# Weight sums of the query, key and gate products made beside the products, in three token blocks in place of two

## The chip, the cores and the metric

The kernel runs on one core of a Trainium2 chip. The metric is the time of one execution on the device in microseconds (us); lower is better. The engines of the core are TensorE (PE in the profile, with its weight loads as PEld), VectorE (DVE), ScalarE (ACT), GpSimd (POOL) and SyncE (SP), whose queue issues all the DMAs here.

## The reference

One inference step of two layers over 2048 prompt tokens and 64 sample tokens (8 requests of 8 tokens). The change lies in layer 1, the retention layer:

```python
p = _rmsnorm(x, norm_w) @ w_in                       # (L,1024) @ (1024,6144)
q, k, v, gate = jnp.split(p, [1024, 2048, 4096], axis=-1)
q = _rotary(q.reshape(B, L, 4, 256), pos0)
k = _rotary(k.reshape(B, L, 4, 256), pos0) * 256 ** -0.5
v = v.reshape(B, L, 4, 512)
o, S = _retention_chunked(q, k, v, S0)               # per head: S = s_dec*S + k^T v, o = q S + (q k^T * D) v
o = _rmsnorm(o, onorm_w) * jax.nn.silu(gate.reshape(B, L, 4, 512))
y = x + o.reshape(B, L, 2048) @ w_out                # then a final rmsnorm
```

Layer 0 (gated delta rule) runs before it and is not touched.

## The kernel before

Layer 1 takes the prompt in four blocks of 512 tokens (n = 0 to 3), and in each block the four heads (h = 0 to 3) one after the other; block 0 carries the 64 sample tokens along. I call the work of one block and head a stage, (n,h). A stage has, in program order: the gate, query and key products, the rotation of query and key, the value product, the output product of the stage before (`flush_B`, `outproj_B`), and then a task `ret_prompt` is added to a planner `pipe`. `pipe.pump()`, called between products, lets such tasks emit their next instructions; so the chain of head h (four chunks of 128 tokens, `kT`, `ap`, `o`, `p` on PE, with the state `Sr` between chunks) runs among the products of the next stage. In block 0 a second task `ret_sample` follows each `ret_prompt`: it fans out the sample values `vraw` by eight DMAs, makes a key tile `K3`, and works through 16 states that are loaded, updated (`ps` on PE, then DVE) and stored. The tile framework sets each engine's final order at build time; an engine then takes its instructions strictly in that order.

Every matrix product is made of three passes of rounded numbers: a weight is split into a high part (a copy on ACT, `L210`) and a low part (a subtraction on DVE, `L211`).

Blocks 0 and 1 make plain products: eight weight loads of 512 KB for gate, query and key, four for the values. Blocks 2 and 3 (`n >= FIRST7`) make each 2x2 block product from seven products of quarters (`quad`, `vquad`, `seven`) in place of eight. For that the tokens' side needs sums of quarters (`build_halves`, DVE and ACT) and the weights' side four sums for each of six weight pairs and head. `prep` makes these sums during blocks 0 and 1: 2 x 24 units, each with a load (`Rw`), four sums on POOL (`Sm`), a split on ACT and DVE, and two stores into the DRAM buffer `wh_d`. `wstream` then delivers the seven weight quarters of a product in the order of its job numbers x: 0, 1, 3 are plain quarters (loaded into `wraw` and split), 4 to 7 are the sums (loaded from `wh_d` straight into a weight tile). A weight tile holds two quarters and there are three of them, so the weights run at most six products ahead. At the end of block 1 the program waits in the planner for the rest of `prep` (`pipe.wait(*ptask)`) and then builds the halves of block 2.

Tiles with one tag share buffers in program order: the later one waits until the last reader of the earlier one is done. `p0`, `p1`, `p2` are such tags. In block 0 `p2` holds `vraw` and then `K3`; from block 1 on `p0` to `p2` serve as extra buffers for `xr`, the residual of the output product. `wraw` has two buffers.

Of the kernel before, what the change touches and what calls it, by code (L numbers as in the profile page):

```python
# [10 lines left out]
F32 = mybir.dt.float32  # L11
F32R = mybir.dt.float32r
AF = mybir.ActivationFunctionType
ALU = mybir.AluOpType
# [5 lines left out]
BH = 4  # L20
# [61 lines left out]
class _Layer:  # L82
    pb = None
# [8 lines left out]
def tile_hybrid(ctx: ExitStack, tc: tile.TileContext, a: dict, S: int):  # L92
    nc = tc.nc
    V, ACT, PL = nc.vector, nc.scalar, nc.gpsimd
# [47 lines left out]
    x1_d = dr.tile([D, S + NS], F32, name="x1_d")  # L142
    x2_d = dr.tile([D, S + NS], F32, name="x2_d")
    sr_d = dr.tile([BH, 128, 1024], F32, name="sr_d")
    wh_d = [dr.tile([24, 128, 1024], F32, name=f"wh_d{h}") for h in range(BH)]

    def const(name, shape, src, pool=cst):
        t = pool.tile(list(shape), F32, name=name)
# [26 lines left out]

    def xst(name, wide=True):
        if not wide and xn_[1] == 6:
            k = xn_[2] % 6
            xn_[2] += 1
            if k >= 3:  # L180
                return B.pb.tile([128, TB], F32, tag=f"p{k - 3}", name=name)
        else:
            k = xn_[0] % min(xn_[1], 3 if B.pb else 4)
            xn_[0] += 1
        return (pa if k == 3 else sb).tile([128, XC], F32, tag=f"xst{k}", name=name)
# [829 lines left out]
    def quarters(src, vkind):  # L1015

        if vkind:
            q = [[v3(src[j], 512)[:, :, 256 * i : 256 * i + 256] for i in range(2)] for j in range(2)]
            return q[0][0], q[1][0], q[0][1], q[1][1]
        return [src[j][:, 512 * i : 512 * i + 512] for j in range(2) for i in range(2)]  # L1020
# [16 lines left out]
    def prep(u):  # L1037

        pb = B.pb
        tag = ("ta", "tb")[u]  # L1040
        for h, t in ((h, t) for h in range(BH) for t in range(6)):
            src, vkind = quads(h)[t]
            R = pb.tile([128, 4, 256], F32R, tag=tag, bufs=2, name="Rw")
            Sm = pb.tile([128, 4, 256], F32, tag=tag, bufs=2, name="Sm")
            A11, A12, A21, A22 = (R[:, i, :].bitcast(F32) for i in range(4))
            for x, y in zip((A11, A12, A21, A22), halves_of(src, vkind, u)):
                nc.sync.dma_start(x, y)
            yield 10.0
            PL.tensor_tensor(Sm[:, 0], A21, A22, op=ALU.add)
            PL.tensor_tensor(Sm[:, 1], Sm[:, 0], A11, op=ALU.subtract)  # L1050
            PL.tensor_tensor(Sm[:, 2], A11, A21, op=ALU.subtract)  # L1051
            PL.tensor_tensor(Sm[:, 3], A12, Sm[:, 1], op=ALU.subtract)
            yield 10.0
            with behind():
                ACT.copy(R, Sm)
                V.tensor_tensor(Sm.bitcast(F32R), Sm, R.bitcast(F32), op=ALU.subtract)
            yield 8.0
            out = wh_d[h][4 * t : 4 * t + 4].rearrange("x p (l v c) -> p x l v c", l=2, v=2)[:, :, :, u, :]
            nc.sync.dma_start(out[:, :, 0], R.bitcast(F32))
            nc.sync.dma_start(out[:, :, 1], Sm)  # L1060
            yield 8.0

    def wstream(h):

        q = quads(h)
        jobs = []
        for ts in ([0], [1], [2], [3], [4, 5]):
            for x in (0, 4, 5, 1, 6, 7, 3):
                jobs += [(t, x) for t in ts]
        for i in range(0, len(jobs), 2):  # L1070
            w, raw = wtile(), None
            for j, (t, x) in enumerate(jobs[i : i + 2]):
                o = w[:, j, :]
                src, vkind = q[t]
                if x < 4:
                    if raw is None:
                        raw = sb.tile([128, 1024], F32, tag="wraw", bufs=2, name="wraw")
                    d = raw[:, 512 * j : 512 * j + 512]
                    nc.sync.dma_start(v3(d, 256) if vkind else d, quarters(src, vkind)[x])
                    split(o[:, :512], o[:, 512:], d)  # L1080
                else:
                    nc.sync.dma_start(o.bitcast(F32), wh_d[h][4 * t + x - 4])
            for j in range(2):
                yield v3(w[:, j, :], 512)

# [38 lines left out]
    def seven(product, c):  # L1124

        add = lambda e, out, x, y: e.tensor_tensor(out, x, y, op=ALU.add)  # L1126
        ACT.copy(c[0][0], product("b11"))
        ACT.copy(c[1][1], product("t1"))
        add(V, c[0][1], product("t2"), c[0][0])
        add(V, c[0][0], product("b21"), c[0][0])  # L1130
        add(V, c[1][0], product("t3"), c[0][1])
        add(PL, c[0][1], c[0][1], c[1][1])
        add(PL, c[1][1], c[1][0], c[1][1])
        add(V, c[0][1], product("b22"), c[0][1])
        add(V, c[1][0], product("n4"), c[1][0])
# [47 lines left out]
    def ret_prompt(n, h, QR, KR, Vt, GT, OG, S_):  # L1183
        pb = B.pb
        gC = float(gam[h] ** 128)
        rmask = pb.tile([128, 128], F32, tag="rmk", bufs=2, name="rmk")
        nc.sync.dma_start(rmask, a["rmask"][:, h, :])
        for c in range(4):
            tk = slice(c * 128, (c + 1) * 128)
# [56 lines left out]
    def ret_sample(h, QRs, KRs, vraw, GTs, OG):  # L1246
# [52 lines left out]
        for half in range(2):  # L1299
# [31 lines left out]
            on = ret_on(o, h, 2)  # L1331

            def fin(oT, half=half):
                og = pb.tile([128, 4, 32], F32, tag="ogs", name="ogs")
                V.tensor_tensor(og.rearrange("p d (g t) -> p d g t", t=8),
                                oT.rearrange("p d (g s) -> p d g s", s=32)[:, :, :, 0:8],
                                GTs[:, :, 32 * half : 32 * half + 32].rearrange("p d (g t) -> p d g t", t=8),
# [231 lines left out]


PIN = False
FIRST7 = 2
LAT_E = 4.0
LAT_SUB = 51.0
LAT_K = 5.5
# [123 lines left out]
```

## Time and profile before

| | us |
|---|---|
| median of 3 runs | 3385.2 (3381.08 to 3391.85) |
| the profiled execution, its own time | 3395.24 |
| its span from the first to the last instruction | 3393.5 |
| layer 1 stages from (0,3)'s output product to the end | 1951.2 to 3393.5 |

The span is 1.7 us shorter than the execution's own time. Times of the trace are counted from the start of the span. A stage is bounded below by where the output product in it ends on PE, since PE is the engine that is nearly always busy.

### The profile page before, as it was taken

What the parts mean: (1) busy time and instruction counts of PE and PEld (TensorE: products, weight loads), DVE (VectorE), ACT (ScalarE), POOL (GpSimd) and SP (SyncE); (2) the same over time, 40 slices, a digit from 0 to 9 for tenths busy, and PEclk for the clock granted to TensorE, in tenths of its full rate; (3) what the DMA queues carried; (4) which work ended last, traced back from release to release, by engine and by line L of the source; (5) the groups of instructions that cost most, each with busy time, mean ns of one, the idle gap of its engine ahead of it and who ended that gap; (6) DMA issues with size and microseconds to landing.
All of it is one profiled execution on the core that took longest, in us unless ns stands there. A gap on an engine that the chain in (4) does not pass through costs nothing.

```text
span 3393.5 us, 57080 instructions
## 1 busy us (share of the span) xinstructions
PE 3216.8 (95%) x20572; PEld 2769.3 (82%) x20572; DVE 2357.0 (69%) x5218; ACT 1563.8 (46%) x3527; POOL 493.7 (15%) x770
## 2 busy tenths in 40 slices
PE   7999999999999999999999999999969999999997
PEld 6999887778788788788878778688759899889896
DVE  6876878687868868666475766666667567775666
ACT  7655564465435546335243443344344344443443
POOL 1221010001010000011113121222211111011110
PEclk9999999999999999999999999999979999999999
DMA  4333544335443333446767768766678867688665
GB/s 134 94 98 90 175 139 140 125 97 164 128 133 111 95 117 97 139 131 214 246 212 232 238 217 273 244 208 204 199 247 276 273 226 251 228 269 277 222 238 173
DMA packets 408650, 625.60 MB, mean 184 GB/s; under 512 B 119840, under 2 KB 237360, under 8 KB 408368
## 3 DMA queue, kind: packets, MB, share of 16 engines
q1 hardware_dynamic: 408368, 621.96, 57.3%
q8 instruction: 162, 2.65, 0.3%
q14 instruction: 120, 0.98, 0.1%
HBM read 473.04 MB, written 146.68 MB: 183 GB/s over the span
## 4 chain that ended last, share of the span: by engine, by line
PE 66%; DVE 10%; DMA 10%; ACT 6%; issue 4%; POOL 3%; SPq 1%; DVEq 0%; POOLq 0%; ACTq 0%
PE pp L101 37%; PE sq L101 5%; PE pv L101 5%; PE o L101 4%; PE p L101 4%; PE sv L101 3%; PE kyd L101 2%; DMA w<-wh_d 1%; DMA wraw<-in_w_qkg 1%; PE oT L110 1%; DMA x_d<-xr 1%; DVE w L197 1%; DMA wraw<-in_w_v 1%; POOL so L587 1%; DMA out_ret_s<-st 1%
## 5 line engine op out<-in xcount | busy, mean ns | idle before, releaser
L101 PE MATMUL pp<-xn,w 128*128 128x288 f32 (+1 forms) x6224 | 1285.6, 354 | 12.6 <-ACT xn L210 4.7
L101 PEld LDWEIGHTS pp<-xn,w 128*128 128x128 f32 x6224 | 993.4, 189 | 156.2 <-issue 19.3
L101 PE MATMUL pp<-OG,w 128*128 128x512 f32 (+1 forms) x2880 | 589.8, 363 | 35.4 <-DVE xr L1359 28.0
L101 PEld LDWEIGHTS pp<-OG,w 128*128 128x128 f32 x2880 | 487.9, 192 | 119.6 <-DVE xr L1359 28.0
L196 ACT CAST w<-wraw 128x1024 fp32r<-128x1024 f32 x320 | 336.6, 1052 | 383.6 <-PE pp L101 201.5
L197 DVE TENSOR_TENSOR w<-wraw,w 128x1024 fp32r<-128x1024 f32 x320 | 403.0, 1260 | 149.9 <-ACT w L196 141.0
L101 PE MATMUL sq<-xn,w 128*128 128x256 f32 x1536 | 206.2, 284 | 5.8 <-DVE GT L1126 3.3
L101 PEld LDWEIGHTS sq<-xn,w 128*128 128x128 f32 x1536 | 191.4, 188 | 10.4 <-issue 3.8
L101 PE MATMUL pv<-w,xn 128*128 128x512 f32 x768 | 188.5, 398 | 1.9 <-ACT w L196 1.7
L1359 DVE TENSOR_TENSOR xr<-xr,pp 128x512 f32<-128x512 f32 (+1 forms) x160 | 92.4, 592 | 133.6 <-PE pp L101 114.2
L101 PEld LDWEIGHTS pv<-w,xn 128*128 128x128 f32 x768 | 144.2, 189 | 39.5 <-ACT w L196 1.9
L743 DVE SCALAR_TENSOR_TENSOR acc<-pp,cw,acc 128x511 f32<-128x511 f32 (+2 forms) x216 | 160.3, 742 | 20.8 <-ACT acc L740 20.4
L210 ACT CAST w<-wraw 128x512 fp32r<-128x512 f32 x144 | 86.1, 623 | 151.7 <-PE pp L101 50.2
L211 DVE TENSOR_TENSOR w<-wraw,w 128x512 fp32r<-128x512 f32 x144 | 96.9, 688 | 46.7 <-ACT w L210 46.6
L101 PE MATMUL o<-Sc,Qc 128*128 128x512 f32 x360 | 103.1, 411 | 9.0 <-DVE Sc L211 4.7
L1051 POOL TENSOR_TENSOR Sm<-Rw 128x256 f32<-128x256 f32 x48 | 44.0, 917 | 463.9 <-DMA Rw<-in_w_qkg 302.4
L488 DVE TENSOR_TENSOR VP<-VP,tm 128x66 f32<-128x66 f32 (+26 forms) x510 | 106.6, 209 | 4.4
L486 DVE TENSOR_TENSOR tm<-LP,VP 128x66 f32<-128x66 f32 (+26 forms) x510 | 104.6, 205 | 6.1 <-DMA LP<-sl 2.1
L101 PE MATMUL p<-Vh,Kt 128*128 128x512 f32 x384 | 106.7, 409 | 0.7 <-ACT Vh L210 0.7
L1171 POOL TENSOR_TENSOR so<-oss,rsc 128x1 f32<-128x1 f32 x72 | 19.7, 274 | 562.0 <-ACT on L1169 562.0
L110 PE MATMUL oT<-ident,on 128*128 128x128 f32 x432 | 74.7, 280 | 26.8 <-DVE on L588 11.8
L210 ACT CAST OG<-og 128x256 fp32r<-128x256 f32 x192 | 71.7, 405 | 58.8 <-DVE og L643 27.6
(434 smaller groups left out, 5440.5 us busy)
## 6 DMA issues: line engine op xcount, KB each, us to landing
w<-wh_d SPq DMA_DIRECT2D x192, 512.0 KB, 5.6
wraw<-in_w_in_a SPq DMA_DIRECT2D x128, 512.0 KB, 3.5
x_d<-xr SPq DMA_DIRECT2D x160, 256.0 KB, 3.2
wraw<-in_w_qkg SPq DMA_DIRECT2D x64, 512.0 KB, 4.4
xr<-x_d SPq DMA_DIRECT2D x128, 256.0 KB, 4.4
wraw<-in_w_out_b SPq DMA_DIRECT2D x64, 512.0 KB, 4.1
wh_d<-Rw SPq DMA_DIRECT2D x48, 512.0 KB, 3.2
wh_d<-Sm SPq DMA_DIRECT2D x48, 512.0 KB, 3.5
```

The lines of the kernel that those rows point to most:

```text
L101: ins = nc.tensor.matmul(out, lhsT, rhs, start=start, stop=stop)
L110: ins = nc.tensor.transpose(out, x, ident[:p, :p])
L196: ACT.copy(w[:, 0, :], raw)
L197: V.tensor_tensor(w[:, 1, :], raw, w[:, 0, :].bitcast(F32), op=ALU.subtract)
L210: ACT.copy(hi, x)
L211: V.tensor_tensor(lo, x, hi.bitcast(F32), op=ALU.subtract)
L486: V.tensor_tensor(tv, LP[:, m, m + 1 : m + 1 + n].unsqueeze(2).to_broadcast([128, n, ncol]), VP[:, m, 0:ncol].unsqueeze(1).to_broadcast([1 ...
L488: V.tensor_tensor(VP[:, m + 1 : m + 1 + n, 0:ncol], VP[:, m + 1 : m + 1 + n, 0:ncol], tv, op=ALU.subtract)
L587: PL.tensor_tensor(so, so, mhalf[:, :2], op=ALU.pow)
L743: V.scalar_tensor_tensor(acc[:, sh:], ap[:, : TB - sh], cw[:, ct, j : j + 1], acc[:, sh:], op0=ALU.mult, op1=ALU.add)
L1051: PL.tensor_tensor(Sm[:, 2], A11, A21, op=ALU.subtract)
L1359: V.tensor_tensor(xs[:, s:e], xs[:, s:e], p[:, : e - s], op=ALU.add)
```

## The change

Three things happen. `FIRST7` goes from 2 to 1, so block 1 makes seven products as well. `prep` is cut to the two value pairs (t = 4, 5), 2 x 8 units. And the sums for gate, query and key are no longer stored: `wstream` loads a weight pair into the two `wraw` buffers, makes the sums on POOL into two tiles `P` (tags `p2` and `raws`) and in place in `wraw`, and splits all seven quarters on ACT and DVE, for every head of every block anew. In the order of the seven products the two that use plain weight quarters (x = 0 and 1) now come first, and `seven` adds in another order. Three buffers are given up (the second of `rmk`, the one of `ogs`, and `p2` as a buffer for `xr`).

```diff
-    wh_d = [dr.tile([24, 128, 1024], F32, name=f"wh_d{h}") for h in range(BH)]
+    wh_d = [dr.tile([8, 128, 1024], F32, name=f"wh_d{h}") for h in range(BH)]
...
-            k = xn_[2] % 6
+            k = xn_[2] % 5
...
-        for h, t in ((h, t) for h in range(BH) for t in range(6)):
+        for h, t in ((h, t) for h in range(BH) for t in (4, 5)):
...
-            for x in (0, 4, 5, 1, 6, 7, 3):
+            for x in (0, 1, 4, 5, 6, 7, 3):
                 jobs += [(t, x) for t in ts]
+        live = {}
+
+        def ready(t):
+
+            r = [sb.tile([128, 1024], F32, tag="wraw", bufs=2, name="wraw") for _ in range(2)]
+            for x, y in zip(r, q[t][0]):
+                nc.sync.dma_start(x, y)
+            P = [B.pb.tile([128, 512], F32, tag=x, name="P") for x in ("p2", "raws")]
+            A11, A12, A21, A22 = quarters(r, False)
+            PL.tensor_tensor(P[0], A21, A22, op=ALU.add)
+            PL.tensor_tensor(P[1], P[0], A11, op=ALU.subtract)
+            PL.tensor_tensor(A21, A11, A21, op=ALU.subtract)
+            live[t] = {0: A11, 4: P[0], 5: P[1], 1: A12, 6: A21, 7: P[0], 3: A22}
+
+        ready(0)
...
-                if x < 4:
+                if not vkind:
+                    split(o[:, :512], o[:, 512:], live[t][x])
+                    if x == 4:
+                        PL.tensor_tensor(live[t][7], live[t][1], live[t][5], op=ALU.subtract)
+                    if x == 3 and t < 3:
+                        ready(t + 1)
+                elif x < 4:
...
-        ACT.copy(c[0][0], product("b11"))
+        ACT.copy(c[1][0], product("b11"))
+        add(V, c[0][0], product("b21"), c[1][0])
         ACT.copy(c[1][1], product("t1"))
-        add(V, c[0][1], product("t2"), c[0][0])
-        add(V, c[0][0], product("b21"), c[0][0])
+        add(V, c[0][1], product("t2"), c[1][0])
...
-        rmask = pb.tile([128, 128], F32, tag="rmk", bufs=2, name="rmk")
+        rmask = pb.tile([128, 128], F32, tag="rmk", bufs=1, name="rmk")
...
-                og = pb.tile([128, 4, 32], F32, tag="ogs", name="ogs")
+                og = pb.tile([128, 4, 32], F32, tag="A", name="ogs")
...
-FIRST7 = 2
+FIRST7 = 1
```

How the order on the engines moves is seen at three places. The first is PE early in stage (1,0), where `ret_prompt` of (0,3) runs. Before, its chunks (`kT`, `ap`, `o`, `p`) stand between plain products (`pp`):

```order
L101 MATMUL pp_21846<-xn_21511,w 128x512 x3
L101 MATMUL pp_21847<-xn_21511,w 128x512 x3
L101 MATMUL o<-Vh,Ah 128x512 x3
L101 MATMUL p<-Vh,Kt 128x512 x6
L110 MATMUL kT<-ident,KR 128x128 x2
L101 MATMUL ap<-QR,KR 128x128 x2
L101 MATMUL pp_21846<-xn_21511,w 128x512 x3
L101 MATMUL pp_21847<-xn_21511,w 128x512 x3
```

In the changed kernel, at the same place, PE has the first two quarter products (`sq`, 24 matmuls, weights x = 0 and 1), and then the chunks:

```order
L101 MATMUL sq<-xn_21431,w 128x256 x6
L101 MATMUL sq<-xn_21432,w 128x256 x6
L101 MATMUL o<-Vh,Ah 128x512 x2
L101 MATMUL p<-Vh,Kt 128x512 x4
L101 MATMUL ap<-QR,KR 128x128 x2
L110 MATMUL oT<-ident,on 128x128 x3
L101 MATMUL o<-Sc,Qc 128x512
L110 MATMUL oT<-ident,on 128x128
L101 MATMUL o<-Sc,Qc 128x512 x5
L101 MATMUL o<-Vh,Ah 128x512 x3
L101 MATMUL p<-Vh,Kt 128x512 x6
L110 MATMUL kT<-ident,KR 128x128 x2
```

The plain products between the chunks are gone, and so it goes on for 31 rows, of which the last two are the first `os` of `ret_sample`: the third quarter product, whose weight x = 4 is a POOL sum, stands behind all four chunks.

The second place is POOL at the same time. In the changed kernel it has the `so` steps of the chunks of (0,3) (two rows each), the last two of which are shown, and behind them the sums for the first weight pair and the next (`P` and `wraw`):

```order
L1192 TENSOR_TENSOR so<-oss,rsc 128x1
L1193 TENSOR_TENSOR so<-so,mhalf 128x1
L1079 TENSOR_TENSOR P<-wraw 128x512
L1080 TENSOR_TENSOR P<-P,wraw 128x512
L1081 TENSOR_TENSOR wraw<-wraw 128x512
L1093 TENSOR_TENSOR P<-wraw,P 128x512
```

Before, the sums of `prep` (`Sm`) stand there, and no product of block 1 reads them:

```order
L1052 TENSOR_TENSOR Sm<-Rw,Sm 128x256
L1172 TENSOR_TENSOR so<-so,mhalf 128x1
L1171 TENSOR_TENSOR so<-oss,rsc 128x1
L1172 TENSOR_TENSOR so<-so,mhalf 128x1
L1171 TENSOR_TENSOR so<-oss,rsc 128x1
L1172 TENSOR_TENSOR so<-so,mhalf 128x1
L1051 TENSOR_TENSOR Sm<-Rw 128x256
```

So the first sum that block 1 needs has moved behind the last `so` of the chain of (0,3).

The third place is PE later in (1,0), where `ret_sample` of (0,3) updates its states (`os`, `ps`). In the changed kernel the fourth weight pair begins there:

```order
L101 MATMUL sq<-xn_21432,w 128x256 x5
L101 MATMUL os<-st,QRs 32x512 x4
L101 MATMUL sq<-xn_21432,w 128x256
L101 MATMUL ps<-V_22320,Kts 128x512 x2
L110 MATMUL oT<-ident,on 128x128 x4
L101 MATMUL ps<-V_22320,Kts 128x512 x2
L101 MATMUL os<-st,QRs 32x512 x4
L101 MATMUL ps<-V_22320,Kts 128x512 x4
L101 MATMUL sq<-xn_21429,w 128x256 x2
L101 MATMUL sq<-ta,w 128x256 x2
```

Before, the same instructions stand singly among plain products:

```order
L101 MATMUL ps<-V_22213,Kts 128x512
L101 MATMUL pp<-xn_21498,w 128x512
L101 MATMUL ps<-V_22213,Kts 128x512
L101 MATMUL pp<-xn_21498,w 128x512 x3
L101 MATMUL ps<-V_22213,Kts 128x512
L101 MATMUL pp<-xn_21498,w 128x512 x2
L101 MATMUL pp<-xn_21511,w 128x512
L101 MATMUL os<-st,QRs 32x512 x3
```

What moved: the third product of the fourth pair (`sq<-xn_21429` with a summed weight) now stands behind 15 of the 16 state updates, of which the last eight have no products between them.

## Rows read from the trace of the kernel before

**Rows 1.** The page: busy time, share of the span, instructions, by engine.

```profile
PE 3216.8 (95%) x20572; PEld 2769.3 (82%) x20572; DVE 2357.0 (69%) x5218; ACT 1563.8 (46%) x3527; POOL 493.7 (15%) x770
```

**Rows 2.** Windows, (1,0) to (3,0): us; busy PE, PEld, DVE, ACT, POOL; clock; DMA; GB/s.

```profile
1951.20:2111.30 160.10, 153.81 (x852) 126.93 (x851) 100.66 (x161) 66.27 (x121) 26.41 (x36) 1.00 0.75 245
2111.30:2233.70 122.40, 114.11 (x487) 89.58 (x486) 72.47 (x106) 44.89 (x74) 30.47 (x38) 0.96 0.73 236
2233.70:2341.60 107.90, 107.90 (x486) 87.30 (x485) 66.74 (x93) 43.97 (x73) 23.85 (x30) 1.00 0.65 212
2341.60:2506.70 165.10, 131.85 (x566) 103.75 (x565) 112.60 (x179) 71.28 (x134) 38.07 (x50) 0.89 0.61 199
2506.70:2594.90 88.20, 87.46 (x627) 81.86 (x626) 54.53 (x90) 34.30 (x62) 10.50 (x12) 1.00 0.82 275
2594.90:2701.40 106.50, 103.62 (x715) 94.96 (x714) 72.20 (x128) 42.79 (x86) 15.97 (x20) 1.00 0.83 277
2701.40:2804.30 102.90, 101.40 (x703) 93.33 (x702) 64.97 (x115) 41.32 (x84) 13.05 (x18) 1.00 0.71 240
2804.30:2916.40 112.10, 106.89 (x721) 96.78 (x720) 85.61 (x167) 52.62 (x112) 12.62 (x18) 0.98 0.71 238
2916.40:3020.30 103.90, 100.48 (x688) 92.15 (x688) 67.78 (x117) 44.66 (x88) 13.05 (x18) 0.98 0.74 245
```

**Rows 3.** Waits between 2428 and 2507 us: waiting engine and line, releaser, us.

```profile
PE pp L101 <- DVE xr L1359: 22.5, 1, 22.5
```

**Rows 4.** The tile Sm (prep): ns min/median/max, first and last start.

```profile
L1056 DVE TENSOR_TENSOR Sm<-Sm,Rw x48: 1212/1220/1760, 1526.5 to 2473.9; 128x1024 fp32r<-128x1024 f32 x48
```

**Rows 5.** Timeline of PE: start, us, instruction; two quarter products, matmuls of a chunk.

```profile
2856.44 1.59 PE L101 MATMUL sq<-ta,w 128*128 128x256 f32 x12
2857.87 1.59 PE L101 MATMUL sq<-xn,w 128*128 128x256 f32 x12
...
3327.42 1.63 PE L101 MATMUL p<-Vh,Kt 128*128 128x512 f32 x6
```

**Rows 6.** Timeline of PE in (1,3): starts of two chunks with no products between.

```profile
2450.12 0.41 PE L110 MATMUL kT<-ident,KR 128*128 128x128 f32 x2
2459.94 0.44 PE L110 MATMUL kT<-ident,KR 128*128 128x128 f32 x2 [0.58 <-DVE Sr L1230]
```

**Rows 7.** SP's timeline in (1,0): the DMAs that read vraw.

```profile
2017.59 2.69 SPq L1257 DMA_DIRECT2D r<-vraw  x4
2021.09 2.51 SPq L1257 DMA_DIRECT2D r<-vraw  x4
```

**Rows 8.** The tile vraw: DMA times over all of block 0.

```profile
DMA to landing us min/median/max: 2.0/2.1/4.0
```

**Rows 9.** The tile K (K3) and its readers: ns min/median/max, first and last start.

```profile
L1321 ACT ACTIVATE Kts<-K,kms x64: 386/402/424, 1590.0 to 2065.5; 128x128 fp32r<-128x128 f32 x64
L1275 ACT ACTIVATE K<-kTs,kms x4: 678/682/684, 1583.6 to 2028.2; 128x512 fp32r<-128x512 f32 x4
```

**Rows 10.** The tile w on DVE in blocks 2 and 3: ns min/median/max.

```profile
L211 DVE TENSOR_TENSOR w<-wraw,w x142: 677/686/695, 2510.5 to 3301.4; 128x512 fp32r<-128x512 f32 x142
```

**Rows 11.** The tile Vt on POOL: ns min/median/max of a 128x512 operation.

```profile
L1126 POOL TENSOR_TENSOR Vt<-Vt x16: 1279/1506/2164, 2567.8 to 3306.5; 128x512 f32<-128x512 f32 x16
```

**Rows 12.** Timeline of DVE and of POOL, in (1,3): start, us, instruction.

```profile
2454.37 0.68 DVE L211 TENSOR_TENSOR Sc<-Sr,Sc 128x512 fp32r<-128x512 f32 x1
2461.60 1.22 DVE L211 TENSOR_TENSOR Vh<-Vt,Vh 128x512 fp32r<-128x512 f32 x1
...
2462.35 1.05 POOL L1052 TENSOR_TENSOR Sm<-Rw,Sm 128x256 f32<-128x256 f32 x1
```

**Rows 13.** Windows in (2,2): all quarter products of gate, query, key; ten us of it, with chunks.

```profile
2701.30:2760.80 59.50, 58.78 (x437) 55.27 (x436) 42.05 (x86) 32.00 (x71) 9.34 (x16) 1.00 0.66 225
...
2731.30:2741.30 10.00, 10.00 (x72) 9.15 (x71) 8.95 (x19) 7.24 (x16) 2.59 (x4) 1.00 0.33 100
```

**Rows 14.** DMA issues of the page: KB each, median us to landing.

```profile
wraw<-in_w_qkg SPq DMA_DIRECT2D x64, 512.0 KB, 4.4
```

More of the change, by code (lines that the diff above doesn't have):

```diff
@@ L1057, in prep @@
             yield 8.0
-            out = wh_d[h][4 * t : 4 * t + 4].rearrange("x p (l v c) -> p x l v c", l=2, v=2)[:, :, :, u, :]
+            out = wh_d[h][4 * t - 16 : 4 * t - 12].rearrange("x p (l v c) -> p x l v c", l=2, v=2)[:, :, :, u, :]
             nc.sync.dma_start(out[:, :, 0], R.bitcast(F32))
@@ L1078, in wstream @@
                     d = raw[:, 512 * j : 512 * j + 512]
-                    nc.sync.dma_start(v3(d, 256) if vkind else d, quarters(src, vkind)[x])
+                    nc.sync.dma_start(v3(d, 256), quarters(src, True)[x])
                     split(o[:, :512], o[:, 512:], d)
                 else:
-                    nc.sync.dma_start(o.bitcast(F32), wh_d[h][4 * t + x - 4])
+                    nc.sync.dma_start(o.bitcast(F32), wh_d[h][4 * t - 16 + x - 4])
             for j in range(2):
```

## The prediction

> **What bounds the kernel now.** I first read the page for the engine that is nearly always busy: PE, 95% of the span, with DVE second at 69% [rows 1]. A mean over two layers says little, so next come the windows by stage [rows 2]. In (1,2), which makes plain products, PE is busy for all of 107.9 us. In (2,1) and (2,2), with seven products, it is busy for 103.6 of 106.5 and 101.4 of 102.9 us. So in an undisturbed stage PE sets the time, and the time changes by what PE has to do. Two stages stand out. (1,3) lasts 165.1 us with PE busy for 131.9, at a mean granted clock of 0.89; and (1,0), which my window opens with the output product before it, lasts 160.1 with PE busy for 153.8. The list of waits for the end of (1,3) says why: one wait of 22.5 us of the output product for DVE's addition to `xr` [rows 3], while `prep` still runs, up to 2473.9 us [rows 4], and the halves of block 2 are built after it. (2,3), where halves are built without `prep`, lasts 112.1, 9.2 more than (2,2).
>
> **The change, part by part.** I sum against the profiled execution, 3395.24 us (span 3393.5 and 1.7 around it); the median of the three runs is 3385.2, 10 us less, and I carry the difference over to that.
>
> *Block 1 with seven products.* Per stage the plain (1,2) against (2,2): 107.9 - 102.9 = 5.0 us less [rows 2]. (1,2) thus gives -5. (1,1) has beside it the final norm of block 0, and (2,1) that of block 1: 106.5, to which I add 4 for the 64 more columns (an estimate), so 122.4 becomes 110.4, -12. These 12 hold some idle time of PE (122.4 less 114.1), part of which may stay: -5 to -15.
>
> *The end of block 1.* `prep` has 16 units in place of 48. From 1526.5 to 2473.9 us 48 went by, some 20 us each [rows 4]; 16 take about 320, and block 0 still has 425 us to go at the start of them. So nothing is left to wait for, and (1,3) with (2,0), 165.1 + 88.2 = 253.3 us, becomes what (2,3) with (3,0) is, 112.1 + 103.9 = 216.0: -37.3. For the 32 units of splits that vanish I credit nothing more, since where they ran PE had its products as cover.
>
> *The start of block 1.* Here the price lies, and the order of the instructions shows it. Four things come together in (1,0).
> First, halves are now built at the end of block 0: +9, as (2,3) stands over (2,2) [rows 2].
> Second, `P` shares the tag `p2` with `vraw` of (0,3). The first sum, for weight x = 4, cannot start before the eight DMAs have read `vraw`, and these come after the last chunk of `ret_prompt` (0,3), whose buffers they fill. So after two products PE has only the chunks. Two chunk starts with no products between them are 9.8 us apart, with `prep` in DVE's way [rows 6]; without it I take 7.5, and three and a fraction of them: 24.5. Behind them the DMAs take 2.7 + 2.5 us to issue [rows 7] and 2.1 to land [rows 8], the sum 1.3 (a 128x512 operation on POOL took 1.28 to 2.16) [rows 11], and the split some 1.3 (DVE's part 0.69) [rows 10]: 9.9. That makes 34 us, in which PE has some 17 of its own work that it must do anyhow (a chunk has 15 matmuls of 512 columns, six of which take 1.6 [rows 5], and eight small ones: about 4.6, and `ret_sample` begins): +17, from 10 (tighter chunks) to 27 (9.8 us each).
> Third, `K3` shares `p2` as well, so the sums of the fourth pair wait until its last reader is done. `K3` lived from 2028.2 to 2065.5 us, plus 0.4 for the read: 37.7 [rows 9]. Add 2.6 for sum and split; off go six and a half products of 1.43 us [rows 5] and some 7 of `ps` and `os`: 40.3 - 16.3 = 24. With less DMA traffic beside it I take +20, from 12 to 26.
> Fourth, in the catch-up between the two the weights go round a loop: last quarter split, load into `wraw` (4.4 to land [rows 14], about 0.5 to issue), sums, split. That is some 12.5 us a pair where seven products take 10: +3.
> Less the 6.3 of idle that (1,0) already has (about 6), and the 5.0 of the products: 9 + 17 + 20 + 3 - 6 - 5 = +38, from +15 to +60. The wait on the shared tag is queued on POOL, so the `so` and addition steps behind it wait too, and with them the products.
>
> *The sums on POOL, in each of 12 stages.* Per stage 18 splits become 34: 16 x 0.686 = 11.0 us more on DVE [rows 10], and about as much on ACT, which has 41 of 103 us busy [rows 2] and is no bound. DVE goes from 65.0 to 76 of 102.9. Covered by that average is a stretch that is not: while the chunks run, DVE is busy for 8.95 of 10 us [rows 13]. Over the four chunks (some 40 us) 4.2 are free. About 6 of the 16 splits fall in it (4.1), the others ahead of it in the output product or behind it. Beside that, eight of the 16 POOL sums fall in it, and POOL slows DVE: a split of 128x512 took 0.68 us by itself and 1.22 beside `Sm` operations of POOL [rows 12]. Eight times 0.53 is 4.2. So 8.3 us come into 4.2: 4.1 too many, of which a part moves behind. I take 2.5 us a stage, nearer to 4.1 than to nothing, and 11 stages, as (1,0) is priced above: +27, from 0 (all of it hides) to +102 (rival 2).
> What is read of this row has a rule beside it. The Trainium skill (SBUF — State Buffer, "Who interferes with whom") says that VectorE with two SBUF inputs and GpSimd take a shared port as an exclusive lock, so that the loser blocks for the whole instruction. By it each sum could cost DVE its full 1.28 us, an estimate of 16 x 1.28 = 20.5 a stage in place of 8.5 at most; the row agrees that they collide, but shows 0.54 lost beside an operation of 1.05.
>
> *The round trip of the weights in other stages.* The loop of 12.5 us a pair stands against products and chunks of 59.5 / 4 = 14.9 [rows 13], so it is covered by PE's own work; without the chunks (four products of a pair are 10 us) some 2.5 a pair would show. Fewer loads of sums, `wh_d` from 192 to 96 in three blocks, relieve a DMA that nothing waits for: 0. The buffers given up (`rmk`, `ogs`, a sixth for `xr`) I cost at nothing: a `xr` buffer is held for some 10 us and five serve one product in 2.8.
>
> *Sum:* +38 - 12 - 5 - 37.3 + 27 = +11 us: 3406 on the profile's scale, **3396** on that of the median.
>
> **The rivals.**
> 1. *DVE hides all of the sums* (it decides below 1 us a stage): then 38 - 54 = -16, 3369. For it: the mean of 76 of 103 us, and that the order was made with the splits in it. Against: the stretch at 89%.
> 2. *DVE becomes the bound of the seven-product part.* It has 42.05 of 59.5 us [rows 13]; 11.0 more and 16 x 0.53 = 8.5 for collisions make 61.6, and at the 0.895 that DVE reached among the chunks 68.8 us: +9.3 a stage, 102 in place of 27, sum +86, 3471. It decides once DVE is over 90% busy in those 60 us. Against it: splits ahead of and behind the part. The Trainium skill's lock (SBUF — State Buffer, "Who interferes with whom"), taken whole, would give an estimate of 73.6 us in place of 61.6; no row here is that bad.
> 3. *The two waits on `p2` cost little*, 15 us together in place of 37, since the chunks run close and the states' DMAs go faster without `prep`: (1,0) at +16 and the sum at -11, 3374. It decides if `K3` lives under 25 us. Against it: its 37.7 us, which one round of store and load after another makes up.
>
> **How the numbers follow.** Chances: forecast 0.50 (its own range 3376 to 3418), rival 1 0.20, rival 2 0.12, rival 3 0.18. A measurement of this kernel can tell about 0.3%, 10 us, from no change. The forecast at +11 spreads over slower (0.25), same (0.18) and faster (0.07); rival 1 over faster (0.14), same (0.05) and slower (0.01); rival 2 is slower; rival 3 is faster (0.10), same (0.07) or slower (0.01). That makes faster 0.31, same 0.30, slower 0.39. For 8 in 10 the range must reach rivals 1 and 3 with their spread, to 3350, and most of the way to rival 2, to 3455.
>
> **What would show it.** In the profile after: (1,3) with (2,0) near 216 us and no wait of 22 us there; (1,0) near 198, with two stretches in which PE waits, the first ended by a split of `P` after the eight reads of `vraw`, the second after the last read of `K3`; (1,2) near 105; stages of blocks 2 and 3 2 to 3 us longer, with DVE at 80 us or more in each and splits of over 1 us beside POOL's sums. I am wrong if the stages of blocks 2 and 3 grow by more than 6 us or not at all, or if (1,0) keeps its 160.

## The result, and the profile after

The change makes the kernel **slower: 3516.4 us median of 4 runs (3503.8 to 3524.6) against 3384.6, a ratio of 1.038 (1.035 to 1.042)**. Slower was the likeliest sign in the prediction, at a chance of 0.39, but 3396 is 120 us too low, and the range ended at 3455. That the sign is right says little, as +11 us is about what a measurement can tell from nothing.

The profiled execution took 3503.8 us. The windows by stage come first, cut as in [rows 2] (us; busy PE, PEld, DVE, ACT, POOL; clock; DMA; GB/s): (1,0) with the output product before it, then one stage a line up to (3,0).

```profile
1937.10:2134.60 197.50, 163.58 (x1063) 143.49 (x1062) 128.49 (x221) 77.49 (x160) 43.79 (x42) 0.90 0.53 174
2134.60:2251.10 116.50, 107.62 (x709) 95.82 (x708) 88.72 (x144) 50.34 (x101) 40.26 (x37) 0.99 0.55 184
2251.10:2368.40 117.30, 105.03 (x702) 95.49 (x701) 79.77 (x131) 50.73 (x100) 35.65 (x34) 0.97 0.45 152
2368.40:2495.90 127.50, 110.93 (x721) 99.28 (x720) 104.83 (x183) 61.75 (x128) 36.91 (x34) 0.96 0.44 152
2495.90:2610.00 114.10, 101.60 (x688) 92.80 (x688) 85.67 (x132) 53.47 (x104) 35.62 (x34) 0.99 0.47 159
2610.00:2730.00 120.00, 108.09 (x714) 97.38 (x713) 86.83 (x145) 51.64 (x103) 39.19 (x36) 0.97 0.55 183
2730.00:2845.70 115.70, 105.57 (x703) 96.40 (x702) 79.34 (x131) 50.74 (x100) 35.67 (x34) 0.96 0.45 150
2845.70:2970.30 124.60, 108.59 (x719) 97.48 (x717) 102.19 (x181) 61.88 (x128) 35.46 (x34) 0.97 0.46 158
2970.30:3092.00 121.70, 105.54 (x689) 95.13 (x689) 86.47 (x136) 53.83 (x104) 38.54 (x35) 0.94 0.44 147
```

Set beside [rows 2] and the terms of the prediction (2.5 us a stage for DVE included):

| stages | before | predicted | after |
|---|---|---|---|
| (1,0), with the output product ahead | 160.1 | 198 | 197.5 |
| (1,1) | 122.4 | 113 | 116.5 |
| (1,2) | 107.9 | 105 | 117.3 |
| (1,3) and (2,0) | 253.3 | 221 | 241.6 |
| (2,1) to (3,3), seven stages | 780.0 | 797 | 872.0 |

The rows add up to +121.2 us; the two profiled executions differ by 108.5, since the window of (1,0) opens 14.1 us earlier after the change (1937.1 for 1951.2). How much of these 14 the shorter `prep` gives is not shown: in the twelve runs with the short `prep` the window opens anywhere from 1937 to 1955.

(1,0) came out as summed. Every other row with seven products is longer than priced, and the seven stages behind (2,0) make most of it: +92 us where +17.5 was priced. Their windows, before and then after:

```profile
2594.90:3374.90 780.00, 760.14 (x5125) 691.83 (x5123) 526.12 (x943) 330.42 (x673) 99.00 (x137) 1.00 0.73 244
```

```profile
2610.00:3482.00 872.00, 788.82 (x5124) 710.79 (x5122) 635.15 (x1054) 393.57 (x784) 255.94 (x245) 0.96 0.47 160
```

PE's idle time goes from 780.0 - 760.1 = 19.9 to 83.2, and its busy time grows by 28.7 with the same number of matmuls: the granted clock fell from 1.00 to 0.96. DVE gains 109 us of work and is then busy for 73% of the 872.0 us.

What PE waits for in a stage shows in the list of waits of (2,2), 2735 to 2785 us:

```profile
PE sq L101 <- DVE GT L1147: 6.6, 2, 4.4
```

This is the addition in `seven` that empties a PSUM bank, a part of the memory that PE writes its products to; GT holds those of the gate. Over the seven stages PE waits 37.0 us for it, and 4.0 before the change. The timeline ahead of the wait of 4.4 (start, us, engine, instruction), across engines, with the rows between left out:

```profile
2741.56 0.59 ACT L1190 ACTIVATE on<-o 128x512 f32<-128x512 f32 x1
2742.33 1.75 POOL L1081 TENSOR_TENSOR wraw<-wraw 128x512 f32<-128x512 f32 x1
2744.04 0.18 POOL L1192 TENSOR_TENSOR so<-oss,rsc 128x1 f32<-128x1 f32 x1
2744.89 0.69 ACT L1194 ACTIVATE on<-o,so 128x512 f32<-128x512 f32 x1 [2.66 <-POOL so L1193]
2745.98 0.48 DVE L1217 SCALAR_TENSOR_TENSOR Kt<-kT,rsc,Kt 128x256 fp32r<-128x256 f32 x1 [1.86 <-ACT Kt L1216]
2748.61 0.42 DVE L1147 TENSOR_TENSOR GT<-sq,GT 128x256 f32<-128x256 f32 x1
2749.08 1.65 PE L101 MATMUL sq<-xn,w 128*128 128x256 f32 x6 [4.36 <-DVE GT L1147]
```

ACT has read `o` by 2742.2, but `so` stands behind a sum of 1.75 us on POOL. ACT waits at L1194 for `so`, what stands behind it on ACT and DVE is late, and so, by this reading, is the bank (e1 below tests it). After the gap the clock is down (windows of the wait, and of the two stretches of 4 us behind it):

```profile
2744.70:2749.10 4.40, 0.04 (x2) 0.02 (x1) 3.12 (x8) 3.83 (x8) 1.39 (x2) 0.73 0.36 119
2749.10:2753.10 4.00, 4.00 (x13) 3.42 (x14) 1.98 (x4) 2.21 (x4) 1.84 (x2) 0.50 0.00 0
2753.10:2757.10 4.00, 4.00 (x26) 3.46 (x25) 2.47 (x6) 2.77 (x8) 0.86 (x2) 0.95 0.00 0
```

0.50 is the lower of the two levels (1.2 of 2.4 GHz): 13 matmuls in 4 us where the next four have 26. The second wait of the stage (2.2 us, to 2771.7) looks different: there DVE is busy without a break, with splits drawn out beside POOL's sums (rows left out again):

```profile
2766.83 2.61 DVE L211 TENSOR_TENSOR Sc<-Sr,Sc 128x512 fp32r<-128x512 f32 x2
2767.25 1.63 POOL L1080 TENSOR_TENSOR P<-P,wraw 128x512 f32<-128x512 f32 x1
2768.85 1.71 POOL L1081 TENSOR_TENSOR wraw<-wraw 128x512 f32<-128x512 f32 x1
```

The two splits, 0.69 each when alone [rows 10], take 2.61 together. In the page, DVE's splits of sums have a mean of 967 ns (x144), those of plain quarters 707 (x264).

That gave three theories. **A, queue:** POOL works in order, and `so` and the additions stand behind sums that wait for loads. **B, port:** DVE and POOL hinder each other where both read SBUF, the memory of their operands. **C, round trip**, which the prediction priced at 0: two `wraw` buffers hold only one pair, so the next pair's quarters come late. A fourth, **D**, is C's relative: the chained sums themselves come late.

### The profile page after: what moved, and what is told of

It reads as the page before. It is cut to its first block, busy times and chain, and to the rows that moved or that the text cites. A ratio compares the mean times of both kernels' runs of the same rounds, so it can differ in the third digit from the quotient of the medians.

```text
span 3501.8 us, 58924 instructions
## 1 busy us (share of the span) xinstructions
PE 3228.9 (92%) x21436; PEld 2818.2 (80%) x21436; DVE 2536.5 (72%) x5518; ACT 1657.5 (47%) x3767; POOL 692.8 (20%) x874
## 4 chain that ended last, share of the span: by engine, by line
PE 54%; DVE 17%; DMA 9%; ACT 7%; issue 6%; POOL 5%; SPq 1%; POOLq 0%; DVEq 0%; ACTq 0%
PE pp L101 31%; PE sv L101 4%; PE o L101 3%; PE sq L101 3%; PE p L101 2%; PE pv L101 2%; DMA w<-wh_d 2%; DVE w L211 2%; PE kyd L101 2%; DMA wraw<-in_w_qkg 2%; DVE Sc L211 1%; DVE w L197 1%; PE oT L110 1%; POOL P L1079 1%; POOL so L587 1%
## 5 line engine op out<-in xcount | busy, mean ns | idle before, releaser
L101 PE MATMUL pp<-xn,w 128*128 128x288 f32 (+1 forms) x5456 | 1095.5, 348 | 11.1 <-ACT xn L210 4.7
L101 PEld LDWEIGHTS pp<-xn,w 128*128 128x128 f32 x5456 | 849.8, 189 | 118.8 <-issue 16.6
L101 PE MATMUL sq<-xn,w 128*128 128x256 f32 x2304 | 315.8, 289 | 65.5 <-DVE GT L1147 33.9
L101 PEld LDWEIGHTS sq<-xn,w 128*128 128x128 f32 x2304 | 294.4, 193 | 78.7 <-DVE GT L1147 29.0
L210 ACT CAST w<-wraw 128x512 fp32r<-128x512 f32 x264 | 158.8, 622 | 211.2 <-DMA wraw<-in_w_v 68.2
L211 DVE TENSOR_TENSOR w<-wraw,w 128x512 fp32r<-128x512 f32 x264 | 180.7, 707 | 15.7 <-ACT w L210 14.1
L211 DVE TENSOR_TENSOR w<-P,w 128x512 fp32r<-128x512 f32 x144 | 138.4, 967 | 46.6 <-ACT w L210 45.6
L101 PE MATMUL sv<-w,xn 128*128 128x256 f32 x1152 | 145.5, 283 | 12.8 <-DMA w<-wh_d 12.5
L210 ACT CAST w<-P 128x512 fp32r<-128x512 f32 x144 | 88.4, 622 | 143.8 <-POOL P L1079 77.1
L101 PEld LDWEIGHTS sv<-w,xn 128*128 128x128 f32 x1152 | 139.2, 188 | 17.1 <-DMA w<-wh_d 12.7
```

The lines of the kernel that those rows point to most:

```text
L101: ins = nc.tensor.matmul(out, lhsT, rhs, start=start, stop=stop)
L210: ACT.copy(hi, x)
L211: V.tensor_tensor(lo, x, hi.bitcast(F32), op=ALU.subtract)
```

## The experiments

Ratios are to the kernel before, run beside each on the same chip; 1% is 34 us.

| run | median us | ratio to before (95%) |
|---|---|---|
| the change | 3516.4 | 1.038 (1.035 to 1.042) |
| e1 no `so` | 3482.0 | 1.030 (1.027 to 1.033) |
| e2 no sums | 3354.7 | 0.993 (0.991 to 0.995) |
| e3 sums on DVE | 3428.8 | 1.016 (1.013 to 1.019) |
| e4 sums issued later | 3518.4 | 1.041 (1.039 to 1.044) |
| e5 sums unread | 3528.7 | 1.042 (1.040 to 1.044) |
| e6 unread, no `so` | 3501.9 | 1.034 (1.031 to 1.036) |
| e7 sums on DVE, later | 3438.5 | 1.016 (1.014 to 1.018) |
| e8 sums of constants | 3481.3 | 1.028 (1.025 to 1.030) |
| e9 sums of 64 columns | 3405.9 | 1.006 (1.004 to 1.007) |
| e10 memsets for sums | 3427.1 | 1.010 (1.006 to 1.014) |
| e11 block 1 plain | 3437.2 | 1.013 (1.009 to 1.017) |
| b1 before, no `so` | 3364.4 | 0.993 (0.991 to 0.995) |
| b2 before, new order | 3395.0 | 1.002 (0.999 to 1.004) |
| h1 one pair of six in place | 3373.9 | 0.996 (0.995 to 0.998) |
| h2 two pairs of 24 in place | 3384.2 | 0.998 (0.997 to 1.000) |

**e2: without sums.**

```
-            P = [B.pb.tile([128, 512], F32, tag=x, name="P") for x in ("p2", "raws")]
...
-            PL.tensor_tensor(P[0], A21, A22, op=ALU.add)
-            PL.tensor_tensor(P[1], P[0], A11, op=ALU.subtract)
-            PL.tensor_tensor(A21, A11, A21, op=ALU.subtract)
-            live[t] = {0: A11, 4: P[0], 5: P[1], 1: A12, 6: A21, 7: P[0], 3: A22}
+            live[t] = {0: A11, 4: A12, 5: A21, 1: A12, 6: A21, 7: A12, 3: A22}
...
-                        PL.tensor_tensor(live[t][7], live[t][1], live[t][5], op=ALU.subtract)
```

> The changed kernel with the 16 sums of weights of each stage on POOL left out: products 4, 5, 6 and 7 take a plain quarter (A12, A21, A21, A12) in place of a sum; loads, splits, their order and the products stay. Theories A and B alike: all that POOL's sums cost goes, what stays is 5 products fewer and 16 splits more a stage in DVE's shadow: stages of blocks 2 and 3 near 104 to 106 us, the whole 3360 to 3400. Theory C: the stages keep 112 us or more: 3450 to 3500.

Measured 0.993. Its seven stages (2,1) to (3,3):

```profile
2538.60:3327.20 788.60, 765.09 (x5125) 692.51 (x5123) 578.70 (x1054) 389.63 (x783) 97.08 (x137) 1.00 0.51 176
```

788.6 against 780.0: with some 111 splits more, DVE is busy for 52.6 us more (7.5 a stage; the splits of quarters grow by 74.2, other groups shrink), and the kernel loses 1.2 a stage. Loads, `wraw` and order are as in the change; only the two `P` buffers are gone with the sums. C falls. All the rest, 4.5% or some 150 us, comes with the sums and `P`.

**e1 and its control b1: the way over POOL.**

```
-        PL.tensor_tensor(so, ss, B.rsc[:, h, col : col + 1], op=ALU.add)
-        PL.tensor_tensor(so, so, mhalf[:, :1], op=ALU.pow)
-        ACT.activation(on, o, AF.Copy, scale=so)
+        ACT.activation(on, o, AF.Copy, scale=ss)
```

> The changed kernel with the two small POOL instructions of each retention chain left out (L1192, L1193): `on` is scaled by `ss` itself, so the normalisation of the retention's output is left out, and the chain no longer passes through POOL at all; POOL's sums of weights stay as they are. Theory A (queue): those two instructions stand behind sums that wait for a DMA or run 1.3 to 1.8 us each, ACT stands still at `on`, then DVE's additions that empty a PSUM bank come late, and PE waits 4 us or so once a stage; with the clock that falls behind it, 8 to 10 us in each of 11 stages: 3420 to 3450. Theory B (port): the sums make DVE's splits twice as long, wherever the chain goes: 3490 to 3515. Theory C (round trip): the quarters come too late because two `wraw` buffers serve a pair: 3495 to 3515.

> The kernel before with the two small POOL instructions of each chain left out (`on` scaled by `ss`, the normalisation left out): the control for the 27 to 34 us that the same edit took from the change. If those were lost to POOL's sums standing ahead, the kernel before has little to gain: 3370 to 3385. If the way over POOL is slow by itself, it gains as much: 3345 to 3360.

The change gains 0.8% by it, the kernel before 0.7%. In the seven stages the time goes from 872.0 to 862.9 and from 780.0 to 771.7, which is the same. So the step over POOL costs some 8 us there in either kernel, and the wait that the timeline above puts on `so` is not where the change lost its time: without it PE still waits 44.1 us for that addition to GT over the whole kernel, with it 59.5.

**e4: the sums issued later.** `sums(t)` is called behind the split of product 1 in place of `ready(t)`.

> The changed kernel with the three first sums of a pair issued one step later, right behind the split of product 1 in place of behind the loads, so that POOL's queue is not held by a transfer that has not landed (28 us a stage of waiting at L1079); computation whole, the sums' own time stays. Theory A: `so` finds POOL free for most chunks, 3 to 6 us a stage: 3450 to 3490, unless products 4 and 5 then wait for their sums. Theories B and C: 3505 to 3530.

1.041: no gain, but this run does not test the queue. The tile framework put POOL's instructions in the order that they had: in (2,2) and (2,3) POOL's rows are those of the change, one for one, and in the seven stages POOL waits 180.9 us at the first sum for the weights to land, where it waits 172.3 in the change. The run is the change once more.

**e5 and e6: sums that nobody reads.** The third sum goes into `P[1]`; products take plain quarters as in e2.

```
-            PL.tensor_tensor(A21, A11, A21, op=ALU.subtract)
-            live[t] = {0: A11, 4: P[0], 5: P[1], 1: A12, 6: A21, 7: P[0], 3: A22}
+            PL.tensor_tensor(P[1], A11, A21, op=ALU.subtract)
+            live[t] = {0: A11, 4: A12, 5: A21, 1: A12, 6: A21, 7: A12, 3: A22}
```

> The changed kernel with the 16 sums of each stage made on POOL as before, of the same sizes, but read by nobody: the third is written into the second buffer of P and products 4, 5, 6, 7 take plain quarters (A12, A21, A21, A12), so the sums are left out of what is computed. Against the run without sums (3355) it adds POOL's work, its queue and its share of the port, but no split waits for a sum. Theory B (port) with A (queue): the time stays near that of the change, 3470 to 3510. Theory D (latency: ACT and DVE stand in order behind a split that waits for DMA, then for two chained sums of 1.3 to 1.8 us): the time falls to 3360 to 3400.

> The same with the two small POOL instructions of each retention chain left out too (`on` scaled by `ss`, the normalisation left out), so that nothing in the loop over chunks waits for POOL: what POOL's sums still cost is the port alone, and the four additions of GT, QR, KR and Vt. Theory B: within 30 of the run with unread sums, 3450 to 3490. Theory A: 3360 to 3390. Theory D: no difference to the run with unread sums.

e5 loses as much as the change although no split waits for a sum: D falls. e6 gains 0.8% on it, as e1 and b1 do. In e5's list of groups (DVE, 2400 to 3300 us; busy, mean ns, idle before) the splits are drawn out, and so is `Sc`, which has nothing to do with weights. `Sr`, of the same size, is not; one of its two inputs is `p`, in PSUM:

```profile
L211 DVE TENSOR_TENSOR w<-wraw,w 128x512 fp32r<-128x512 f32 x254 | 202.4, 819 | 30.8 <-ACT w L210 30.2
L211 DVE TENSOR_TENSOR Sc<-Sr,Sc 128x512 fp32r<-128x512 f32 x64 | 59.5, 962 | 0.0
L1252 DVE SCALAR_TENSOR_TENSOR Sr<-Sr,p 128x512 f32<-128x512 f32 x64 | 42.7, 682 | 0.6 <-PE p L101 0.6
```

**e8: a test that failed.** Sums of a broadcast column of `mhalf` in place of the weights were to leave nothing of the loss but the port.

> The run with unread sums and no `so`, with one thing more: the sums read a column of constants (`mhalf`, broadcast to 512) and P in place of the weights, so POOL waits for no transfer and holds no buffer of weights, and nothing in the loop over chunks waits for it. What is left out of the computation is as there (sums, normalisation of the retention). POOL's 16 instructions a stage of 128x512 stay as they are. If the port alone makes the rest of the loss, the time stays near that run's 1.034 of before, 3470 to 3505; if holding `wraw` or waiting in POOL's queue for transfers makes it, it falls to 3355 to 3400.

1.028, but for another reason. Bound to no load, the sums ran ahead of their stages: in (1,1) POOL was busy for 164.1 of 221.8 us with 145 instructions, and PE waited 45.0 us for `rr` and 19.6 for GT behind them. From (1,2) on no sums are left and its stages are e2's. So its time says nothing on the port's share. Its (1,1) does show the collision: the splits of quarters there have a mean of 1106 ns, where e2's (1,1) has 713.

**e9 and e10: queue against port.** e9 keeps waits and buffers and cuts each sum of e5 to 64 columns. e10 keeps most of POOL's busy time too, but lets it do next to nothing but write:

```
-            PL.tensor_tensor(P[0], A21, A22, op=ALU.add)
+            PL.tensor_tensor(P[0][:, :1], A21[:, :1], A22[:, :1], op=ALU.add)
+            PL.memset(P[0], 0.0)
+            PL.memset(P[0], 0.0)
```

(and the same for the other three).

> The other half: the unread sums with 64 of 512 columns each, `so` in place, so that POOL's queue is still held by every transfer of weights but its instructions and their share of the port are an eighth (the sums are left out of what is computed). If waiting behind transfers in POOL's queue is what delays `so` and the chain, 3440 to 3490; if it is POOL's busy time and the port, 3355 to 3385.

> The run with unread sums (3529, so 1.042 of before) with each sum cut to its first column and followed by two memsets of the whole 128x512 buffer: POOL waits for the same transfers, holds the same buffers and is busy as long (two memsets of 0.53 us, as the trace has them at L670 and L1536, and 0.2), but it reads next to nothing from SBUF; the sums are left out of what is computed. If the loss is DVE's splits and POOL's sums reading SBUF through one port, the splits beside POOL fall back to 0.68 us and the time to that of the sums of 64 columns, 3395 to 3430. If it is POOL's busy time in its own queue, the time stays at 3500 to 3530.

1.006 and 1.010, against 1.042 for e5. The seven stages of e5, e9 and e10:

```profile
2629.80:3509.80 880.00, 797.33 (x5125) 714.76 (x5123) 645.49 (x1054) 390.43 (x784) 256.27 (x245) 0.96 0.46 158
```

```profile
2572.40:3380.10 807.70, 771.01 (x5124) 695.88 (x5123) 583.21 (x1053) 389.67 (x783) 148.89 (x245) 0.99 0.50 172
```

```profile
2589.10:3414.90 825.80, 775.65 (x5125) 698.42 (x5123) 581.71 (x1053) 388.54 (x783) 242.60 (x461) 0.99 0.50 168
```

POOL is busy for 242.6 us in e10 and 256.3 in e5, and waits for the same loads and buffers; DVE is busy for 581.7 and 645.5, and the time is 825.8 and 880.0. And in e10's list of groups (as for e5) the splits are back:

```profile
L211 DVE TENSOR_TENSOR w<-wraw,w 128x512 fp32r<-128x512 f32 x272 | 187.9, 713 | 44.1 <-ACT w L210 43.3
...
L211 DVE TENSOR_TENSOR Sc<-Sr,Sc 128x512 fp32r<-128x512 f32 x64 | 43.4, 701 | 7.0 <-ACT Sc L210 6.9
```

So of the 91.4 us that unread sums cost in seven stages (880.0 - 788.6), 54.2 go once POOL only writes (B). POOL's 13.7 us less of work in e10 would be some 3 of them, an estimate at the rate of e10 against e9. Another 18.1 are what e10 has over e9, by POOL's longer time in its queue, and 19.1 what e9 has over e2. These 19.1 are not one thing: POOL is held by loads and holds buffers, but it is also busy for 51.8 us more than in e2 and still reads an eighth of the columns. PE's wait for the additions to GT goes with the time: 3.8 us in e2's seven stages, 14.7 in e9's, 20.6 in e10's, 35.4 in e5's. For the 18.1 a wait on DVE shows as well: it stood 22.2 us for POOL's additions of GT in e10's seven stages, 8.5 in e9's and 8.3 in e2's. Over the whole kernel the three parts are 3.2%, 0.5% and 1.2%. The intervals of e9 and e10 overlap, and the profiled executions of e2 and e10 lie 7 us below and 9 above their medians, so the two smaller parts are rough.

**e3 and e7: the sums on DVE**, behind the loads as in the change, or later as in e4 (`PL` becomes `V`).

> The changed kernel with the 16 sums of each stage made on DVE in place of POOL, the computation whole. Adds 16 x 0.69 = 11 us of DVE a stage (79 to 90 of some 105), takes away the queue on POOL and the port's share. Theories A and B: stages of blocks 2 and 3 lose 5 to 10 us each: 3400 to 3450. Theory C, or DVE as the bound of the seven-product part: the same or longer than the change, 3510 to 3580.

> The changed kernel with the 16 sums on DVE and the three first of a pair issued behind the split of product 1, so that DVE's queue is not held by a transfer; computation whole. Against the sums on DVE behind the loads (3429): if DVE's standing behind the DMA is what is left of the cost, 2 to 4 us a stage come back, 3385 to 3410; if DVE's 11 us more of work a stage are the cost, no change, 3420 to 3440.

1.016 for both. In e7 DVE waits less for loads at its sums, 9.2 us in the seven stages for 14.0 in e3, and gains nothing by it. The same sums cost 2.2% over e2 on DVE, 4.5% on POOL, although DVE is the busier engine. The seven stages of e3:

```profile
2581.90:3406.10 824.20, 776.54 (x5122) 698.58 (x5120) 645.68 (x1163) 389.14 (x783) 105.76 (x137) 0.99 0.49 169
```

DVE is as busy here as in e5 (645.7 and 645.5 us), and the time is 55.8 us shorter. So the sum of DVE's work by itself does not set the loss.

**e11 and b2: the parts of the change.** `FIRST7 = 2` in the change; the order of products alone in the kernel before.

> The changed kernel with the blocks of seven products cut back to two (the last), block 1 with eight plain products as before the change; sums in place, computation whole. Block 1 was priced by the stages of both traces: (1,0) with the projection before it +37, (1,1) -6, (1,2) +9, and (1,3) now without the wait for preparation either way. Some 35 to 45 us less than the change, 3465 to 3490: two thirds of the loss stay in the 8 stages of blocks 2 and 3. If block 1 is the loss, 3390 to 3420.

> The kernel before with the change's order of products alone (plain quarters of products 0 and 1 first, and the additions that go with it), everything prepared as before. All theories: no difference, 3375 to 3395.

b2: no difference. e11 gains 2.5%, twice the expected. Its stages (1,0) to (1,3), this time without the output product ahead, take 125.2, 110.8, 107.8 and 111.7 us, where the change has 160.8, 116.5, 117.3 and 127.5; the halves at the end of block 0 are no longer built either. Its seven stages take 870.9, as in the change (872.0), so what is lost there does not come from block 1. Its (1,1) is also 11.6 shorter than before the change, with the same plain products. That `prep` of the weights of queries, keys and gates no longer runs beside it is the likely cause, not tested alone.

**h1 and h2: a version that beats both.** Block 1 plain; all pairs prepared but the fourth (h1), or but the fourth of heads 2 and 3 (h2), which are summed on DVE.

```
-        for h, t in ((h, t) for h in range(BH) for t in (4, 5)):
+        for h, t in ((h, t) for h in range(BH) for t in (0, 1, 2, 4, 5)):
...
-                if not vkind:
+                if t in (3,):
```

> A version between the two: block 1 plain as before the change, five of six pairs of a head prepared during blocks 0 and 1, and only the fourth (K) summed in place, on DVE, behind the split of product 1; the order of products is that of the change; computation whole. 80 in place of 96 prepared halves should end the wait for the preparation at (1,3) (some 37 us of the 253 of (1,3) and (2,0)); four sums a stage cost a quarter of what sixteen cost on DVE, about 1 us in each of 8 stages. 3345 to 3375; if the preparation is not what (1,3) waits for, 3380 to 3400.

> As the version with one pair of six summed in place, but only for heads 2 and 3 (two of the 24 pairs of weights), the other 22 prepared as before the change; computation whole. Heads 0 and 1 lose the 1 to 2 us a stage that four sums on DVE cost. If 88 prepared halves are few enough to end before (1,3) does, 3355 to 3372; if (1,3) waits again for the last halves, 3375 to 3390.

h1 is 0.4% faster than before. Its (1,3) and (2,0):

```profile
2346.60:2458.20 111.60, 111.60 (x507) 90.22 (x506) 82.18 (x142) 51.48 (x99) 7.20 (x12) 1.00 0.52 173
2458.20:2561.10 102.90, 99.71 (x687) 91.16 (x687) 72.29 (x126) 46.86 (x92) 12.53 (x18) 1.00 0.69 231
```

214.5 us, where the prediction had 216.0 without the wait for `prep`. Its seven stages take 796.0, 16 more than before, with four sums a stage on DVE. h2 prepares too much: its (1,3) is 132.4, part of the wait is back.

## Why the prediction was wrong

- **The step that failed is "The sums on POOL, in each of 12 stages"**: 2.5 us a stage, of a range that ended at 102 for 11 stages. The seven undisturbed stages grew by 13.1 each, past the 6 that the prediction itself named as a sign of being wrong. Its sizes were not short. DVE's splits were put at 11.0 a stage, and all 16 collisions, of which the forecast used half, at 16 x 0.53 = 8.5; measured are 10.6 for the splits of quarters (7.5 for DVE as a whole, e2) and (635.2 - 578.7) / 7 = 8.1. What failed is the cover. "8.3 us come into 4.2 ... of which a part moves behind" treated DVE as a store of free time. But in the traces DVE, ACT and POOL each take their instructions in order, so a split drawn out among the chunks makes the addition behind it late, and with it the PSUM bank (PE's wait for the additions to GT: 20.6 us in e10, 35.4 in e5). How much of DVE's added work comes out as time depends on what it is: 16% for e2's splits (8.6 of 52.6 us), 53% for e3's sums (35.6 of 67.0), and 85% for the collisions, if all that e10 saves against e5 is put down to them (54.2 of 63.8).
- **Two fifths were left out of that step**: outside (1,0), POOL's own queue was priced at nothing. What is left of the sums when POOL only writes is 37.2 us in seven stages (e10 less e2), 5.3 each. `so` in it is no more than a small part (e1 and b1 gain alike; e6 gains 18.1 in its seven stages on e5, 10 more than b1 does, but its profiled execution lies 13 us below its median). POOL's additions to GT show for the 18.1 of busy time. Why the same additions come late in e9, its 19.1, stays open.
- **The clock was left out**: of the 92 us, 63.3 are PE's gaps and 28.7 PE's own work, the same number of matmuls at a mean granted clock of 0.96 in place of 1.00 (e2, still at 1.00, has 5.0 of the 28.7).
- **Rival 2 (DVE as the bound, +9.3 a stage, 3471)** had the right place and side and two thirds of the size, at a chance of 0.12, but not the mechanism. Its condition was not met: over the first 60 us of (2,2) after, DVE is busy for 74%. Only slices are full (14.38 of 15 us from 2760 on), and with DVE as busy as in e5, e3 is 55.8 us shorter.
- **The Trainium skill** (SBUF — State Buffer, "Who interferes with whom") was weighed on its lock and set aside for the row's 0.54. The same section says that a VectorE instruction with two SBUF inputs contends with a GpSimd one that reads SBUF, not with one that only writes. The runs agree: a split has a mean of 819 ns in e5, beside sums, and 713 in e10, beside memsets, and an operation with one input in PSUM takes 682 in e5, for 679 without sums in e2.
- **(1,0): +38 against +37.4, right, though not in each part.** The two stretches in which PE waits are there: PE's share falls to 9.4 and 7.4 of 15 us around 1998 and 2058, and POOL's sums start only behind the eight reads of `vraw` (the last issued at 2000.9) and the last read of `K3`:

```profile
2003.27 1.27 POOL L1079 TENSOR_TENSOR P<-wraw 128x512 f32<-128x512 f32 x1 [5.21 <-DVE V L1281]
...
2069.52 1.26 POOL L1079 TENSOR_TENSOR P<-wraw 128x512 f32<-128x512 f32 x1 [14.82 <-ACT Kts L1342]
```

  The first row names DVE's `V`, which is done by 2002.9. The last reads of `vraw` land at about the same time (ACT waits for them until 2003.04), and it is these that the shared tag makes the sum wait for. By runs, with the output product ahead: 160.1 before, 168.0 in e2 (no `P` at all), 184.8 in e9 (waits on the tags and transfers), 198.2 in e5. So +8 for halves less products, +17 for held queue and tags, +13 for sums as such; the prediction had +37 for the tags. That the total fits is in part luck.
- **The end of block 1, -37.3, was right by itself**: 216.0 was priced for (1,3) and (2,0) with seven products, and e2, which has them without the sums, takes 218.4 (h1, with plain products in (1,3), 214.5). In the change the per-stage loss takes it back to 241.6.
- **The round trip, priced at 0, was right** (e2). That the vanished `prep` gives nothing beside PE's products was wrong, if it is what makes e11's (1,0) and (1,1) 6 and 12 us shorter than before. The -12 that the sum gave to seven products in (1,1) are there with plain products too.

## What to carry to other kernels

A gap on an engine that works in order is no cover by its size: ask which instruction stands behind the one that is moved in, and who waits for that. Work moved to an idle GpSimd is not free where VectorE reads two SBUF operands beside it; here the same sums cost half on the busier VectorE. And a wait that the timeline shows is a candidate, not a cause: the control, the same cut in the kernel before, is what showed that `so` was not it. An edit of the program's order is a test only if the engines' order in the trace has changed; e4's had not.

## What the runs showed of the hardware

Collisions follow what is read, not how long POOL is busy: with POOL busy for 243 us of the seven stages, some 114 of them in 216 memsets, the mean split of DVE stayed at 0.71 us, and with 256 us, 159 more than without sums, it took 0.82. A small instruction can suffer most: the splits of 128x128 took 0.29 us at the median, and one beside a sum 1.35. The gaps in PE's work also lowered its granted clock, from a mean of 1.00 to 0.96; PE's busy time grew by 28.7 us, a third of what the seven stages lost.
